# First layer's first norm: sums of squares and Newton steps moved from VectorE to GpSimd, and its statistics put ahead of the modulation blocks

## The chip, the core and the metric

The kernel runs on one core of one Trainium2 chip. The metric is the device time of one execution in microseconds. Of the kernel before there are three timed runs and one execution under the profiler. Engines are named as in the profile: PE (TensorE), DVE (VectorE), ACT (ScalarE), POOL (GpSimd), SP (SyncE, which only issues transfers here).

## The reference

One inference step of a two-layer diffusion trunk for 128 context tokens and 512 latent tokens (the kernel holds them as 640 columns), model width 1024. Cut to what the change touches:

```python
def _rms(x):
    xf = x.astype(F32)
    return xf * lax.rsqrt(jnp.mean(xf * xf, axis=-1, keepdims=True) + EPS)

def modulate(x, shift, scale):
    return (_rms(x) * (1.0 + scale.astype(F32)) + shift.astype(F32)).astype(x.dtype)

def modulation(cond, w_mod, b_mod):
    m = jax.nn.silu(cond) @ w_mod + b_mod
    m = m.reshape(m.shape[0], 1, N_MOD, D_MODEL)
    return tuple(m[:, :, i] for i in range(N_MOD))
```

Each layer computes the modulation (six vectors of 1024: shift, scale and gate for two sub-layers). Then it takes the modulated norm of the tokens and one input projection of it (`w_in`), whose columns go to three mixers side by side: a two-directional state-space scan, a latent attention and a gated MLP. An output projection and a gated residual follow, and then a second modulated norm and a gated convolutional feed-forward network (width 2816) with its residual.

## The kernel before

The residual stream `xT` lies in SBUF with the model dimension on the partitions: eight blocks (`KT`) of 128 rows by 640 token columns. Matmuls are made as three products of high and low halves (`mm3`, L146 to L148); the normed input is therefore two tiles, `hh` and `hl`.

**The modulation.** `mod_blocks` (L237 to L275) multiplies SiLU(cond), `sT`, with `w_mod`. For layer 0 it makes five blocks of 512 outputs here, each from four loads of 512 KB into tiles `raw` (L263, eight buffers in this stage), four products a load (L266). After a block, ACT copies its PSUM (`modev`, L272, one buffer); PE transposes it (`modt`, L152), DVE reduces it (`modred`, L245) and adds the bias (`mod`, L250, and L252 for the scales). The function is a generator: each `next` gives one of these twenty loads with its products.

**The norm.** `norm_stats` (L326) squares the eight blocks of `xT` on ACT (the first into `nacc`, L333, the others into `nsq`, L336, two buffers), adds seven times on DVE (L337), sums over the partitions with products against ones (`nst`, L346), makes `nv` on DVE (L349) and calls `rsqrt`: a first guess from the bits (`rs_y`, L104) and three Newton steps on DVE (L109, L111, L112: nine instructions). `bcast` then spreads the result as a diagonal (`dg`, DVE, L373) and products with ones (`nbc`, PE, L376). `norm_apply` goes through the eight blocks: `nt` (DVE, L358), `hh` (ACT, L362), `hl` (DVE, L363). The tokens are normed in two halves, columns 0 to 320 in `begin_layer` (L1676), 320 to 640 at the head of `mixers` (L847), whose `rest` makes the second half's broadcast and apply. `begin_layer` has, for layer 0,

```python
            for _ in range(8):
                next(modulate)
            r = self.norm_stats(N, 0, 320)
            for _ in range(2):
                next(modulate, None)
```

**What comes behind.** The input projection's part that gives tokens by rows is `wtok` (L905 to L907: wth·hh, wtl·hh, wth·hl), the part that gives columns is `win` (L146 to L148). Beside it the tables of the state-space scan are built: rotations `Tr` (POOL, complex products at L91 to L96, in chains, stored by a DMA `Td`, L673), products `G` (L91 to L96) and `Q` (L612 to L616) on DVE and POOL, and from `Q` the `tap` products on PE (L637 to L640), which ACT and DVE turn into `we` (L642, L643) and store. POOL's first rotation chain stands behind a memset of `uT` (L875). The scan's first instruction on DVE is `m` (L749).

**What sets the order.** The program is written in one stream; a scheduler puts each engine's instructions in an order of its own, by a simulated timeline, and that order is what the engine runs, one behind the other. So a small edit can move instructions far from it. Semaphores make an instruction wait for its inputs and for its buffers.

Of the kernel before, what the change touches and what calls it, by code (L numbers as in the profile page):

```python
# [14 lines left out]
OP = mybir.AluOpType  # L15
# [8 lines left out]
NT = 642  # L24
# [14 lines left out]
def spans(lo, hi):  # L39
    out = []  # L40
    if lo < 512:
        out.append((lo, min(hi, 512), 0))
    if hi > CX:
        out.append((max(lo, CX), hi, 1))
    return out


class Trunk:
# [263 lines left out]
                (nc.scalar if g else nc.sync).dma_start(out=dst[:, c], in_=o[:, c])  # L312


    def norm(self, pool, l, which, lo, hi, hh, hl):

        r = self.norm_stats(pool, lo, hi)

        def rest():
            pb = self.pz("nbc")  # L320
            self.bcast(pool, *r, pb)
            self.norm_apply(pool, l, which, lo, hi, hh, hl, pb)

        return rest

    def norm_stats(self, pool, lo, hi):  # L326

        nc = self.nc
        n = hi - lo
        acc = pool.tile([128, 322], F32, name=self.uid("nacc"), tag="nacc", bufs=2)  # L330
        for k in range(KT):
            if k == 0:
                nc.scalar.activation(acc[:, :n], self.xT[:, k, lo:hi], AF.Square)  # L333
            else:
                sq = pool.tile([128, 322], F32, name=self.uid("nsq"), tag="nsq", bufs=2)
                nc.scalar.activation(sq[:, :n], self.xT[:, k, lo:hi], AF.Square)  # L336
                nc.vector.tensor_tensor(acc[:, :n], acc[:, :n], sq[:, :n], op=OP.add)  # L337
        blocks = []
        for a, b, _ in spans(lo, hi):
            blocks += list(range(a, b - 127, 128))  # L340
            if (b - a) % 128:
                blocks.append(b - 128)
        nb = len(blocks)
        ps = self.pz("nst")
        for i, b in enumerate(blocks):
            nc.tensor.matmul(ps[:, i:i + 1], acc[:, b - lo:b - lo + 128], self.ones[:, 0:1],  # L346
                             start=True, stop=True)
        v = self.smt([128, nb], f"nv{nb}")
        nc.vector.tensor_scalar(v, ps[:, :nb], 1.0 / D, EPS, op0=OP.mult, op1=OP.add)  # L349
        return self.rsqrt(v, nb), [b - lo for b in blocks]  # L350

    def norm_apply(self, pool, l, which, lo, hi, hh, hl, pb):
        nc = self.nc
# [484 lines left out]
    def mixers(self, l, M, n1, N, hh, hl, fill):  # L838

        nc, V, A, I, tc = self.nc, self.nc.vector, self.nc.scalar, self.I, self.tc  # L840
# [3 lines left out]
        def mt(s, sh, dt=F32):  # L844
            return M.tile(list(sh), dt, name=self.uid(s), tag=s, bufs=1)

        rest = self.norm(N, l, 0, 320, NT, hh, hl)  # L847
        yc = mt("yc", [128, 5, 256])
        yA = mt("yA", [128, 2, NT])
        ssc = mt("ssc", [128, 5])  # L850
# [96 lines left out]
        v = win.tile([128, 5, 256], F32, name=self.uid("v"), tag="v")  # L947
        sq = win.tile([128, 256], F32, name=self.uid("vsq"), tag="vsq")
# [88 lines left out]
        for kt in range(6):  # L1037
            c = kt * 128 if kt < 5 else 128 + CX
            ps = self.pb("kv")
            for nb in range(2):  # L1040
                po = ps[:, nb]
                n = slice(nb * 512, (nb + 1) * 512)
# [12 lines left out]
        for tt in (4, 0, 1, 2, 3):  # L1055
            cs = slice(TOK[tt], TOK[tt] + 128)
            ps = self.pb("q")
            for nb in range(2):
                po = ps[:, nb, :384]
                n = slice(nb * 384, (nb + 1) * 384)  # L1060
# [25 lines left out]
        N = n2.enter_context(tc.tile_pool(name=f"n2{l}", bufs=1, side=sb))  # L1086
        fh, fl = self.norm_out(FH)
        self.project_b(l, vt, yh, yl, lambda: self.norm(N, l, 3, 0, 322, fh, fl)())
        rest = self.norm(N, l, 3, 322, NT, fh, fl)
# [585 lines left out]
    def begin_layer(self, l, modulate=None):  # L1675

        tc = self.tc
        self.sides = ("left", "right") if l == 0 else ("right", "left")
        es, n1 = ExitStack(), ExitStack()
        M = es.enter_context(tc.tile_pool(name=f"mix{l}", bufs=1, side=self.sides[0]))  # L1680
        hh, hl = self.norm_out(M)
        N = n1.enter_context(tc.tile_pool(name=f"n1{l}", bufs=1, side=self.sides[0]))
        if modulate:
            for _ in range(8):
                next(modulate)
            r = self.norm_stats(N, 0, 320)
            for _ in range(2):
                next(modulate, None)
            pb = self.pb("nbc")[:, 0]
            self.bcast(N, *r, pb)  # L1690
            for _ in modulate:
                pass
            self.norm_apply(N, l, 0, 0, 320, hh, hl, pb)
        else:
            self.norm(N, l, 0, 0, 320, hh, hl)()
        return es, n1, M, N, hh, hl
# [66 lines left out]
```

## Time and profile before

| | |
|---|---|
| Timed runs (3) | median 1823.65 us, 1820.12 to 1824.7 us |
| The profiled execution: its own time | 1824.9 us |
| Its span | 1823.1 us |
| PE busy | 1692.0 us (93%) |
| DVE busy | 1153.1 us (63%) |
| ACT busy | 680.8 us (37%) |
| POOL busy | 325.0 us (18%) |
| Mean granted TensorE clock | 0.949 of full speed |

The span is that of the trace, from the first instruction to the last; the execution's own time is 1.8 us longer, for what lies around it. It is 1.25 us above the median of the three runs. Busy shares are means over the whole span: in most of it (the feed-forward networks) PE has nine tenths and more; the change lies in the first 160 us, where the shares are others.

### The profile page before, as it was taken

Reading aid. Unit: us, or ns where it says so; the run is one execution under the profiler, and the core shown is the slowest. Engines: PE = TensorE matmul, PEld = TensorE weight load, DVE = VectorE, ACT = ScalarE, POOL = GpSimd, SP = SyncE. Lnnn points to the kernel's source line nnn. Section 1 sums busy time; section 2 is a strip of 40 time slices with the busy share of each in tenths; the row PEclk is TensorE's granted clock in tenths of the full one; section 3 lists DMA queues with packets and bytes.
Section 4 is the critical chain, followed back from the end, with each engine's and each line's share of the span. In section 5 each row is a group of like instructions: output and inputs, shape, how many; then the busy total and the mean of one; then the engine's idle time right before and its main releaser. Section 6 shows DMA issues by size and latency. Waiting matters only on the chain.

```text
span 1823.1 us, 28986 instructions
## 1 busy us (share of the span) xinstructions
PE 1692.0 (93%) x11248; PEld 1510.0 (83%) x11248; DVE 1153.1 (63%) x2377; ACT 680.8 (37%) x1210; POOL 325.0 (18%) x792
## 2 busy tenths in 40 slices
PE   5877889999999999999999878999989999999998
PEld 3767755469889999999999876455989999999998
DVE  6895875667674546456566568565786464555564
ACT  4343454433442424224244346343344132332241
POOL 2896300000186060540000130000000000000000
PEclk7888889899999999999999888989999999999999
DMA  9274453301443523223122543540223131321221
GB/s 283 85 186 119 132 164 123 114 13 58 129 146 116 162 56 117 72 85 110 37 88 67 161 109 105 169 132 1 70 70 93 36 104 47 93 90 39 82 82 58
DMA packets 217577, 182.48 MB, mean 100 GB/s; under 512 B 33438, under 2 KB 202204, under 8 KB 217440
## 3 DMA queue, kind: packets, MB, share of 16 engines
q1 hardware_dynamic: 194736, 154.33, 28.3%
q0 software_dynamic: 8272, 23.87, 4.5%
q10 hardware_dynamic: 14432, 2.44, 0.7%
q8 instruction: 89, 1.46, 0.3%
q14 instruction: 48, 0.39, 0.1%
HBM read 161.94 MB, written 18.64 MB: 99 GB/s over the span
## 4 chain that ended last, share of the span: by engine, by line
PE 74%; DVE 10%; DMA 7%; ACT 4%; issue 2%; POOL 2%; ACTq 0%; SPq 0%; DVEq 0%; POOLq 0%
PE up L146 11%; PE up L148 11%; PE up L147 10%; PE dn L146 5%; PE dn L148 5%; PE dn L147 5%; PE o L1294 3%; PE mod L266 2%; DMA raw<-w_mod 2%; PE wo L146 2%; PE wo L148 2%; PE wo L147 2%; DMA raw<-ffn_w_up 1%; PE s L1274 1%; DMA raw<-w_in 1%
## 5 line engine op out<-in xcount | busy, mean ns | idle before, releaser
L146 PE MATMUL up<-hh,whi 128*128 128x322 f32 x1408 | 435.1, 314 | 10.0 <-ACT hh L362 4.0
L148 PE MATMUL up<-hh,wlo 128*128 128x322 f32 x1408 | 438.1, 312 | 1.8 <-DVE wlo L123 1.5
L147 PE MATMUL up<-hl,whi 128*128 128x322 f32 x1408 | 436.9, 311 | 0.0
L146 PEld LDWEIGHTS up<-hh,whi 128*128 128x128 f32 x1408 | 264.9, 189 | 16.2 <-ACT whi L122 6.4
L148 PEld LDWEIGHTS up<-hh,wlo 128*128 128x128 f32 x1408 | 266.3, 189 | 4.0 <-DVE wlo L123 3.4
L147 PEld LDWEIGHTS up<-hl,whi 128*128 128x128 f32 x1408 | 267.2, 190 | 0.6 <-issue 0.4
L123 DVE TENSOR_TENSOR wlo<-raw,whi 128x1024 fp32r<-128x1024 f32 (+1 forms) x116 | 145.7, 1257 | 140.5 <-ACT whi L122 138.8
L148 PE MATMUL dn<-gh,dl 128*128 128x322 f32 (+1 forms) x704 | 217.9, 311 | 0.5 <-DVE dl L123 0.5
L147 PE MATMUL dn<-glo,dh 128*128 128x322 f32 (+1 forms) x704 | 218.0, 311 | 0.0
L146 PE MATMUL dn<-gh,dh 128*128 128x322 f32 (+1 forms) x704 | 209.9, 312 | 2.3 <-DVE cv L1548 1.8
L1508 DVE SCALAR_TENSOR_TENSOR xT<-dn,mod,xT 128x320 f32<-128x320 f32 (+2 forms) x288 | 112.1, 435 | 127.7 <-PE dn L148 127.6
L122 ACT CAST whi<-raw 128x1024 fp32r<-128x1024 f32 (+1 forms) x116 | 120.6, 1041 | 155.8 <-PE up L147 57.0
L1539 ACT ACTIVATE cv<-up,prm,cw 128x321 f32<-128x321 f32 x88 | 54.2, 620 | 246.7 <-PE up L148 244.4
L148 PEld LDWEIGHTS dn<-gh,dl 128*128 128x128 f32 x704 | 133.3, 189 | 0.7 <-DVE dl L123 0.7
L146 PEld LDWEIGHTS dn<-gh,dh 128*128 128x128 f32 x704 | 131.2, 190 | 2.8 <-issue 2.0
L147 PEld LDWEIGHTS dn<-glo,dh 128*128 128x128 f32 x704 | 133.0, 189 | 0.0
L1540 DVE SCALAR_TENSOR_TENSOR cv<-up,cw,cv 128x320 f32<-128x320 f32 x88 | 48.3, 549 | 63.8 <-ACT cv L1539 62.4
L266 PE MATMUL mod<-raw,sT 128*32 128x256 f32 x768 | 64.5, 432 | 23.4 <-DMA raw<-w_mod 21.4
L123 DVE TENSOR_TENSOR dl<-raw,dh 128x1024 fp32r<-128x1024 f32 x44 | 53.9, 1225 | 45.2 <-ACT dh L122 44.9
L122 ACT CAST dh<-raw 128x1024 fp32r<-128x1024 f32 x44 | 46.1, 1048 | 58.1 <-DMA raw<-ffn_w_down 50.0
L1257 DVE TENSOR_REDUCE nml<-mx 128x1 f32<-128x640 f32 x64 | 51.0, 820 | 23.9 <-PE mx L1255 23.6
L266 PEld LDWEIGHTS mod<-raw,sT 128*32 128x32 f32 x768 | 19.9, 115 | 53.0 <-DMA raw<-w_mod 25.5
(479 smaller groups left out, 3445.4 us busy)
## 6 DMA issues: line engine op xcount, KB each, us to landing
raw<-w_mod SPq DMA_DIRECT2D x96, 512.0 KB, 4.6
raw<-ffn_w_up SPq DMA_DIRECT2D x88, 512.0 KB, 4.0
raw<-ffn_w_down SPq DMA_DIRECT2D x44, 512.0 KB, 3.5
raw<-w_in SPq DMA_DIRECT2D x10, 512.0 KB, 6.5
we<-WEd POOLq DMA_DIRECT2D x8, 512.0 KB, 4.4
qt<-Qd POOLq DMA_DIRECT2D x8, 512.0 KB, 5.1
raw<-w_out SPq DMA_DIRECT2D x16, 256.0 KB, 5.3
raw<-w_out SPq DMA_DIRECT2D x8, 512.0 KB, 3.4
```

What stands on the lines that cost most here:

```text
L122: self.nc.scalar.copy(hi, raw)
L123: self.nc.vector.tensor_tensor(lo, raw, hi.bitcast(F32), op=OP.subtract)
L146: mm(ps, wh, xh, start=start, stop=False)
L147: mm(ps, wh, xl, start=False, stop=False)
L148: mm(ps, wl, xh, start=False, stop=stop)
L266: nc.tensor.matmul(ps[j * 32:j * 32 + 32, c0:c0 + 256], self.sT[:, k0 + j, :], rv[:, j, :], start=k0 == 0, stop=k0 == 4)
L1257: V.tensor_reduce(nm[:, tt:tt + 1], pb[:, :, :320], axis=AX.XY, op=OP.max, negate=True)
L1274: mm(ps, kh[i][:, kc_], qh[i], start=True, stop=False)
L1294: mm(pb[i * 64:(i + 1) * 64, 0], Vt[:, kt, 2 * p + i], Ps[i][kt], start=kt == 0, stop=kt == 4)
L1508: self.nc.vector.scalar_tensor_tensor(self.xT[:, m, a:b], po[:, a - lo:b - lo], self.modcol(l, gi, m, c), self.xT[:, m, a:b], op0=OP.mult, ...
L1539: A.activation(z[:, 0:321], po[:, 0:321], AF.Identity, bias=b, scale=c1)
L1540: V.scalar_tensor_tensor(z[:, 1:321], po[:, 0:320], c0, z[:, 1:321], op0=OP.mult, op1=OP.add)
```

## The change

`norm_stats` and `norm` take an engine `E`. With GpSimd, the seven additions and the Newton steps run there. `rsqrt` had a branch for GpSimd already, which has twelve instructions in place of nine (L109, L114, L115, L116, three times) and tile names with a `p` at the end (`rs_t3p`, `rs_y3p`); the first guess `rs_y03p` stays on DVE. Both halves of layer 0's first norm use it. In `begin_layer` the statistics are written ahead of all modulation loads, and ten loads stand between them and the broadcast. The other norms keep DVE. All sizes and formulas stay.

```diff
-    def norm(self, pool, l, which, lo, hi, hh, hl):
-
-        r = self.norm_stats(pool, lo, hi)
+    def norm(self, pool, l, which, lo, hi, hh, hl, E=None):
+
+        r = self.norm_stats(pool, lo, hi, E)
...
-    def norm_stats(self, pool, lo, hi):
+    def norm_stats(self, pool, lo, hi, E=None):

         nc = self.nc
+        E = E or nc.vector
...
-                nc.vector.tensor_tensor(acc[:, :n], acc[:, :n], sq[:, :n], op=OP.add)
+                E.tensor_tensor(acc[:, :n], acc[:, :n], sq[:, :n], op=OP.add)
...
-        return self.rsqrt(v, nb), [b - lo for b in blocks]
+        return self.rsqrt(v, nb, E), [b - lo for b in blocks]
...
-        rest = self.norm(N, l, 0, 320, NT, hh, hl)
+        rest = self.norm(N, l, 0, 320, NT, hh, hl, nc.gpsimd if l == 0 else None)
...
         if modulate:
-            for _ in range(8):
-                next(modulate)
-            r = self.norm_stats(N, 0, 320)
-            for _ in range(2):
+            r = self.norm_stats(N, 0, 320, self.nc.gpsimd)
+            for _ in range(10):
                 next(modulate, None)
```

The scheduler's orders around it. In the order's rows a name ends in its buffer's number, an operation is `output<-inputs`, and `x4` means four in a row. Lines of the changed kernel lie one higher than those of the kernel before from L329 on.

**Place 1, PE, from its first products with the modulation's weights.** Before:

```order
L266 MATMUL mod_452<-raw_474,sT 32x256 x4
L346 MATMUL nst_511<-ones,nacc_488 128x1 x3
L266 MATMUL mod_452<-raw_480,sT 32x256 x4
L266 MATMUL mod_530<-raw_531,sT 32x256 x4
L152 MATMUL modt_537<-ident,modev_486 128x128 x4
```

```order
L376 MATMUL nbc_551<-dg_552,ones 128x128 x3
L266 MATMUL mod_571<-raw_593,sT 32x256 x4
L266 MATMUL mod_571<-raw_599,sT 32x256 x4
L152 MATMUL modt_607<-ident,modev_605 128x128 x4
L346 MATMUL nst_679<-ones,nacc_656 128x1 x3
L905 MATMUL wtok_875<-wth_853,hh_418 128x288
```

Now:

```order
L152 MATMUL pa_325<-ident,rows_49_329 128x66
L347 MATMUL nst_448<-ones,nacc_425 128x1 x3
L266 MATMUL mod_470<-raw_471,sT 32x256 x4
L266 MATMUL mod_470<-raw_477,sT 32x256 x4
```

```order
L152 MATMUL modt_581<-ident,modev_572 128x128 x4
L906 MATMUL wtok_881<-wth_859,hh_418 128x288
L907 MATMUL wtok_881<-wtl_860,hh_418 128x288
...
L266 MATMUL mod_574<-raw_590,sT 32x256 x4
L908 MATMUL wtok_881<-wth_859,hl_419 128x288
...
L266 MATMUL mod_574<-raw_602,sT 32x256 x4
```

The first half's `nst` stood behind seven loads' products and stands now ahead of all twenty. The broadcast stood behind 18 loads' products and stands behind 11 now, followed by two more; 22 `wtok` products stand among the last three loads, where before all `wtok` products came behind the last load. On ACT, the third to seventh square of the first half (`nsq_433` to `nsq_445`) now stand behind four small loads `dcol` (L632); before, six of the seven stood ahead of those, and the seventh between them.

**Place 2, POOL and DVE, at the second half's Newton steps and broadcast.** POOL before (its first Newton row comes far behind these):

```order
L875 MEMSET uT_708 128x16
L573 MEMSET bs_1028 128x16
L625 MEMSET dcol_1086 128x1
L661 MEMSET Tr_1116 128x4
```

POOL now; between the rows that are shown lies the first rotation chain:

```order
L876 MEMSET uT_714 128x16
...
L91 TENSOR_TENSOR Tr_1122<-Tr_1122,rho 128x4
L93 TENSOR_TENSOR Tr_1122<-Tr_1122,rho 128x4
...
L109 TENSOR_TENSOR rs_t3p_690<-rs_y03p_688 128x3
...
L95 TENSOR_TENSOR G_1040<-G_1040,tm_186_1020 128x256
L96 TENSOR_TENSOR G_1040<-G_1040,tm_187_1021 128x256
L674 DMA Td_287<-Tr_1122 128x328
L674 DMA Td_288<-Tr_1122 128x328
L116 TENSOR_TENSOR rs_y3p_691<-rs_t3p_690,rs_y3p_691 128x3
```

DVE now, at the second half's broadcast:

```order
L364 SCALAR_TENSOR_TENSOR hl_419<-nt_646,mod_91,hh_418 128x320
L374 TENSOR_TENSOR dg_734<-ident,rs_y3p_691 128x384
L359 SCALAR_TENSOR_TENSOR nt_739<-xT,mod_91,nbc_733 128x192
L359 SCALAR_TENSOR_TENSOR nt_743<-xT,mod_91,nbc_733 128x128
L613 TENSOR_TENSOR tm_251_1636<-pw,CT_1633 128x288
```

The second half's twelve Newton instructions stand spread through POOL's first rotation chain, and the last of them behind the chain's two stores. DVE's `dg` needs that last one, and all that DVE does later stands behind `dg`. Ahead of the `uT` memset POOL now has 14 additions and the first half's twelve Newton instructions.

**Place 3, PE, at the last taps of the tables.** Before, they stood among the `win` products (19 products, 8 rows of taps, 26 products, 16 rows of taps):

```order
L640 MATMUL tap_1088<-Q_192_1049,bs_1028 32x112
L146 MATMUL win_2424<-hh_418,whi_2419 128x320
...
L148 MATMUL win_2511<-hh_418,wlo_2507 128x320
L637 MATMUL tap_1954<-Q_299_1941,bs_1894 32x112
```

Now:

```order
L638 MATMUL tap_1960<-Q_299_1947,bs_1900 32x112
...
L641 MATMUL tap_1094<-Q_192_1055,bs_1034 32x112
L1118 MATMUL gm_1587<-v_1420,wsT_1565 128x320
L1118 MATMUL gm_1592<-v_1420,wsT_1565 128x320
L146 MATMUL win_2430<-hh_418,whi_2425 128x320
```

All taps of layer 0 now stand ahead of the first `win` product of 320 columns.

## Rows read from the trace of the kernel before

**Rows 1.** The chain of work that ended last: shares of the span by engine.

```profile
PE 74%; DVE 10%; DMA 7%; ACT 4%; issue 2%; POOL 2%; ACTq 0%; SPq 0%; DVEq 0%; POOLq 0%
```

**Rows 2.** Windows: length, busy PE, PEld, DVE, ACT, POOL, PEclk, DMA, GB/s.

```profile
25.00:50.00 25.00, 17.33 (x130) 6.30 (x130) 23.64 (x110) 7.60 (x15) 0.00 (x0) 0.62 1.09 349
75.00:100.00 25.00, 21.77 (x147) 18.71 (x147) 23.77 (x72) 10.70 (x34) 21.86 (x73) 0.93 0.29 86
125.00:150.00 25.00, 19.22 (x153) 18.08 (x154) 17.28 (x36) 8.85 (x23) 21.30 (x49) 0.86 0.58 149
```

**Rows 3.** DVE's groups by line and shape, 15 to 70 us: busy, mean ns.

```profile
L337 DVE TENSOR_TENSOR nacc<-nacc,nsq 128x322 f32<-128x322 f32 x7 | 3.4, 487 | 0.2 <-ACT nsq L336 0.2
L337 DVE TENSOR_TENSOR nacc<-nacc,nsq 128x320 f32<-128x320 f32 x7 | 3.4, 483 | 1.2 <-ACT nsq L336 1.1
L109 DVE TENSOR_TENSOR rs_t<-rs_y 128x3 f32<-128x3 f32 x6 | 1.2, 208 | 0.0
```

**Rows 4.** Timeline, first norm and modulation: start, length, instruction, [idle before <-releaser].

```profile
25.19 1.08 PE L266 MATMUL mod<-raw,sT 128*32 128x256 f32 x8 [5.22 <-DMA raw<-w_mod]
29.30 1.02 ACTq L631 DMA_DIRECT2D dcol<-ssm_d  x2
30.36 0.83 ACT L336 ACTIVATE nsq<-xT 128x322 f32<-128x322 f32 x2 [0.66 <-DVE nacc L337]
36.67 1.44 PE L346 MATMUL nst<-ones,nacc 128*128 128x1 f32 x6 [0.45 <-DVE modred L245]
50.38 1.06 PE L376 MATMUL nbc<-dg,ones 128*128 128x128 f32 x6 [1.85 <-DVE dg L373]
51.36 1.94 PE L266 MATMUL mod<-raw,sT 128*32 128x256 f32 x16
57.01 0.44 PE L905 MATMUL wtok<-wth,hh 128*128 128x288 f32 x1
57.25 0.44 PE L906 MATMUL wtok<-wtl,hh 128*128 128x288 f32 x1
```

**Rows 5.** Timeline of POOL, first rotation chain and products G.

```profile
53.39 0.12 POOL L875 MEMSET uT<- 128x16 f32 x1 [2.05 <-PE mod L266]
53.70 1.41 POOL L91 TENSOR_TENSOR Tr<-Tr,rho 128x4 f32<-128x4 f32 x1
55.52 0.20 POOL L92 TENSOR_TENSOR tr<-Tr,rho 128x4 f32<-128x4 f32 x1
66.23 0.65 POOL L91 TENSOR_TENSOR G<-pw,bb 128x256 f32<-128x256 f32 x1
73.60 0.85 POOL L96 TENSOR_TENSOR G<-G,tm 128x256 f32<-128x256 f32 x1
124.71 0.95 POOL L96 TENSOR_TENSOR G<-G,tm 128x256 f32<-128x256 f32 x1
```

**Rows 6.** Timeline of POOL, the same Newton steps in another norm.

```profile
178.56 0.32 POOL L115 TENSOR_SCALAR rs_t5p<-rs_t5p 128x5 f32<-128x5 f32 x1
178.96 0.25 POOL L116 TENSOR_TENSOR rs_y5p<-rs_t5p,rs_y05p 128x5 f32<-128x5 f32 x1
```

**Rows 7.** Timeline of DVE, the second half's broadcast and apply.

```profile
64.74 0.66 DVE L373 TENSOR_TENSOR dg<-ident,rs_y 128x384 f32<-128x384 f32 x1
68.73 0.67 DVE L358 SCALAR_TENSOR_TENSOR nt<-xT,mod,nbc 128x192 f32<-128x192 f32 x2 [2.72 <-PE nbc L376]
72.13 2.47 DVE L363 SCALAR_TENSOR_TENSOR hl<-nt,mod,hh 128x192 fp32r<-128x192 f32 x2 [2.73 <-ACT hh L362]
```

**Rows 8.** Timeline, the last taps on PE and what DVE makes of them.

```profile
138.12 0.58 PE L637 MATMUL tap<-Q,bs 128*32 128x112 f32 x2 [5.78 <-POOL Q L616]
145.68 0.24 DVE L643 SCALAR_TENSOR_TENSOR we<-id,dcol,we 128x16 f32<-128x16 f32 x1 [5.22 <-ACT we L642]
153.11 0.23 DVE L643 SCALAR_TENSOR_TENSOR we<-id,dcol,we 128x16 f32<-128x16 f32 x1 [5.20 <-ACT we L642]
157.25 0.83 DVE L749 TENSOR_TENSOR m<-E,T 128x656 f32<-128x656 f32 x1
```

## The prediction

> **What bounds the kernel now.** I read the chain of waits first, then windows of 25 us over the stretch that the change touches, then the timelines of its engines. PE has 74% of the chain [rows 1], but that is the mean of the span. At 25 to 50 us another picture stands [rows 2]: PE is busy 17.33 of 25 us at a granted clock of 0.62, between the two levels 1.2 and 2.4 GHz; DVE is busy 23.64; the transfers run at 349 GB/s. Here loads of `w_mod` and DVE set the pace. From 75 to 100 us DVE (23.77) and POOL (21.86) are both nearly full, and at 125 to 150 us POOL still has 21.30 while DVE has fallen to 17.28. Those two build the tables of the scan, and PE waits for them: a tap waits 5.78 us for POOL's Q [rows 8]. So up to the scan's first instruction at 157.25 us [rows 8] the end is set by two queues, DVE's and POOL's, and what is put late on either shows in the time unless a later wait gives way. Behind the scan come the feed-forward networks, where PE is full and nothing can be made up.
>
> **DVE gets lighter.** Its fourteen additions take 483 to 487 ns each, 6.8 us together, and eighteen Newton instructions at some 208 ns add 3.7 [rows 3]; these durations overlap a little, so the queue gains perhaps 7.5 us. All of that lies before 66 us. It shortens the end only if what DVE does next is there earlier, and the next points say that it is not.
>
> **PE starts later.** The first product of the modulation runs at 25.19 us [rows 4], as its load lands. Now the first half's `nst` stands ahead of it, and that needs seven additions on POOL, whose third to seventh square stand behind four `dcol` loads on ACT. Before, the last two of these were issued from 29.30 for 1.02 us, to 30.32 [rows 4]; a `dcol` waits there for other transfers, not for anything that the change removes. One square is 0.83 / 2, some 0.45 us [rows 4]. The additions on POOL have no row; the nearest are additions and products of 256 columns, 0.65 us, 0.85 and, with DVE busy beside them, 0.95 [rows 5]. By 320/256 that is 0.81 to 1.19 us. I take 0.85, since the first few of them have little beside them, and keep both ends: five additions are 4.05 to 5.95, taken 4.3. Since `nsq` has two buffers, the squares cannot run ahead. 30.3 + 0.45 + 4.3 = 35.1, then `nst`, 1.44 [rows 4]: the first modulation product at 36.5, 11.3 late. PE had idled for loads before, 7.7 of the 25 us [rows 2], and by 36.5 the eight buffers are full; that recovers part. The work that PE did from 25.19 to 53.30 (the end of the last modulation products, 51.36 + 1.94) is 17.33 - 1.44 for `nst`, + 1.06 + 1.94 [rows 2, 4] = 18.9 us. To that come the 22 `wtok` products that stand among the last loads now, at 57.25 - 57.01 = 0.24 each [rows 4], 5.3. The last modulation product thus ends at T0 = 36.5 + 18.9 + 5.3 = 60.7, where it was 53.3: 7.4 late. Bounds: 55, if loads and clock run as well as they can (twelve loads of 512 KB behind the first eight are 18 us at 349 GB/s, from 37.5), and 64, if PE stays at its lower clock throughout or `wtok` waits for `hl`.
>
> **The second half's norm.** POOL's `uT` memset waits for that last product (53.39 before) and its chain with the G products ends at 73.60 + 0.85 = 74.45 [rows 5], 21.1 us later. Now twelve Newton instructions stand in this chain; on POOL one takes 0.25 us, or 0.40 from start to start [rows 6], 0.20 for the chain's own small ones [rows 5]: 2.4 to 4.8, I take 2.6, for most stand between others of the same length. The first operation of the chain took 1.41 and not 0.20 us [rows 5]; that start was paid earlier now, with the first addition: -1.2. So the chain and the last Newton step end at 60.7 + 21.1 + 2.6 - 1.2 = 83.2. On POOL that is 8.7 late for all its later work. On DVE `dg` comes then; it ran at 64.74 [rows 7]. With 0.66 for `dg`, 1.06 for `nbc` [rows 4], 0.67 for two `nt` and 0.5 for `hh`, the first `hl` of the second half is at 86.1; before, 72.13 [rows 7]. DVE's queue behind it is 14.0 late: the 7.5 us won are spent as a wait.
>
> **What gives way.** Before, DVE waited 5.22 and 5.20 us at two `we` [rows 8], because their taps stood among `win` products on PE; those taps stand ahead of all of them now, so these waits can close. If one does, DVE's 14.0 becomes 8.8; POOL's 8.7 stays, since its own idle is small. Both queues then arrive 8.7 late at the scan. The sum: 1824.9 + 8.7 = 1833.6 for the profiled execution, which lies 1.25 above the median; so **1832.4 us**. A measurement of this kernel tells about 0.3% (5.5 us) from no change.
>
> The unknown ends around it: T0 from 55 to 64 is -5.7 to +3.3, the Newton steps -0.2 to +2.2, and 0 or both waits closed instead of one is +5 or, as far as POOL lets it, nothing. That case has 0.38 with 1829 to 1840.
>
> **Rivals.**
>
> 1. *No change: all of it is absorbed* (0.25). For it: DVE has 7.7 and POOL 3.7 us idle from 125 to 150 us [rows 2], the two `we` waits are 10.4, and PE's tap wait of 5.78 [rows 8] is a wait for the same queues. If T0 comes at 57 and POOL's rows, which stretched from 0.65 to 0.95 with DVE beside them [rows 5], run faster while DVE waits, POOL is 3 late and DVE 9 - 10.4, and the time is 1824.9 - 1.25 + 0 to 3, about 1825. Against it: DVE and POOL are full from 75 to 100 us, so nothing is taken back there.
>
> 2. *Faster: the taps' new place decides* (0.15). Both `we` waits close, 10.4 us off DVE, and the second norm is no more than some 5 late, since T0 is at 55 and POOL's chain loses its stretch. Then the scan comes 10.4 - 5 = 5.4 earlier and the time is 1818.2. It decides this way if the second `dg` runs before 72 us or so and POOL's last Q is not later than before. Against it: T0 at 55 with 21 us of POOL behind it puts `dg` at 77; it needs the chain to shrink by 5.
>
> 3. *POOL's last table comes later still* (0.12). POOL's last Q stands behind more of its fourth rotation chain than before; PE waited for POOL at the taps already [rows 8], and now all `win` products queue behind that. Some 6.5 us more of chain on top of 8.7: about 1839.
>
> 4. *DVE and POOL shut each other out* (0.10). In the rows an operation on one engine is only stretched by the other: POOL's G products took 0.65 to 0.95 [rows 5], and no DVE row stood still for a whole POOL instruction. The Trainium skill ("SBUF — State Buffer", section "SBUF: two separate sides") says otherwise: the port pair that the two share is locked for a whole instruction, and the loser, such as a DVE operation with two SBUF inputs against a POOL operation that reads SBUF, blocks fully. As a mechanism of this kernel: if each of the fourteen additions of 0.85 us held up DVE's queue for its length, DVE would lose 12 us where it gained 7.5, the first half's `dg` would come some 3 us later than PE is ready for it, and `wtok` and the last loads with it. T0 would be 63.7 and the time 1835.4. DVE is busy 23.64 of 25 us there [rows 2], so nothing would hide it; for it speaks also that the stretch exists at all.
>
> **How the numbers follow.** The forecast, 3 and 4 are slower, 0.60 together; no change has 0.25, faster 0.15. The likeliest value is 1832.4. The range reaches down to rival 2 with a little beside it, 1817, and up over rival 3, 1841; it leaves out T0 late with rival 3 at once, and a larger gain than 7 us, for which I see no row.
>
> **What would show it.** Right: PE's first `mod` near 36 us and not 25; the `uT` memset on POOL near 60; second `dg` on DVE near 83 with a long wait for POOL's last L116; the two waits before `we` smaller; the scan's first `m` near 166. DVE's busy time from 25 to 50 us falls, and it buys nothing. Wrong: a first `mod` before 32 us (then the squares did not wait for `dcol`, or the additions are cheaper); a T0 below 56; a second `dg` before 75; or an `m` at 157 or earlier although `dg` is late, which would mean that the tables' end was set by something that I have not seen, a transfer for instance.

## The result and the profile after

The changed kernel takes 1846.45 us (median of four runs, 1841.82 to 1850.85) against 1821.88 for the kernel before beside it: a ratio of 1.0136, 95% interval 1.0112 to 1.0160, so 20 to 29 us slower. The forecast had the sign and the chain of steps up to 84 us, and a third of the size: 8.7 us, 1832.4, with 1841 as the upper end. The profiled execution took 1848.79 us (span 1847.0).

The same windows as [rows 2], of the kernel after:

```profile
25.00:50.00 25.00, 9.78 (x98) 5.08 (x98) 24.97 (x83) 8.30 (x17) 18.21 (x24) 0.62 0.86 272
75.00:100.00 25.00, 13.66 (x71) 10.85 (x70) 14.68 (x40) 6.99 (x20) 23.12 (x71) 0.86 0.15 49
125.00:150.00 25.00, 15.05 (x117) 13.45 (x117) 20.37 (x32) 8.68 (x26) 24.49 (x48) 0.86 0.85 220
```

From 25 to 50 us PE does 9.78 us of work in place of 17.33, and DVE is no emptier for what it lost, but fuller: 24.97. From 75 to 100 us DVE, full before, falls to 14.68; it waits for POOL. From 125 to 150 us POOL has no gap left, while PE and its 19.22 have become 15.05.

The steps on their engines, from the timelines of the kernel after (start, length, instruction, [idle before <-releaser]); they answer to [rows 4, 5, 7]:

```profile
37.42 1.44 PE L347 MATMUL nst<-ones,nacc 128*128 128x1 f32 x6 [18.19 <-POOL nacc L338]
38.79 4.49 PE L266 MATMUL mod<-raw,sT 128*32 128x256 f32 x40
63.11 0.13 POOL L876 MEMSET uT<- 128x16 f32 x1 [12.26 <-PE mod L266]
83.33 0.56 DVE L374 TENSOR_TENSOR dg<-ident,rs_y3p 128x384 f32<-128x384 f32 x1 [13.80 <-POOL rs_y3p L116]
```

PE's first `mod` stood at 25.19 and was forecast at 36.5; it is at 38.79. `uT` went from 53.39 to 63.11 (forecast 60.7), the second `dg` from 64.74 to 83.33 (forecast 83.2), with the wait of 13.80 us for POOL in front of it. Up to here the forecast holds to 2.5 us. That `dg` comes on the number itself is luck: `uT` is 2.4 us late, and from `uT` to `dg` it takes 20.2 us in place of the 22.5 forecast. Now the last tables, which answer to [rows 8], first on POOL:

```profile
116.14 1.15 POOL L674 DMA_DIRECT2D Td<-Tr  x2 [0.30 <-POOL Tr L96]
123.36 0.10 POOL L662 MEMSET Tr<- 128x4 f32 x1 [6.08 <-DMA Td<-Tr]
156.72 2.05 POOL L617 TENSOR_TENSOR Q<-tm,tm 64x288 f32<-64x288 f32 x2
```

POOL stood still for 6.08 us until the stores `Td` of its third chain had ended, before it could begin the fourth. In the kernel before it made Q products in that time; now all of the last Q products stand behind the fourth chain's start. POOL's last Q ends at 158.8, before at 139.1. DVE's last Q ends at 159.1, before at 146.9, and by the profile it is for one of DVE's that PE's late taps wait (first the row of the kernel before, then two of the kernel after):

```profile
145.95 0.94 DVE L616 TENSOR_TENSOR Q<-tm,tm 64x288 f32<-64x288 f32 x2
...
157.66 1.43 DVE L617 TENSOR_TENSOR Q<-tm,tm 64x288 f32<-64x288 f32 x2
158.25 0.55 PE L638 MATMUL tap<-Q,bs 128*32 128x112 f32 x2 [3.82 <-DVE Q L617]
```

So both engines' last tables come at about the same time. Then DVE, from the last two `we` to the scan, with some rows between:

```profile
163.06 0.23 DVE L644 SCALAR_TENSOR_TENSOR we<-id,dcol,we 128x16 f32<-128x16 f32 x1 [3.21 <-ACT we L643]
165.17 0.23 DVE L644 SCALAR_TENSOR_TENSOR we<-id,dcol,we 128x16 f32<-128x16 f32 x1 [1.87 <-ACT we L643]
...
173.32 0.36 DVE L1136 TENSOR_TENSOR krg<-kra,k_normr 128x192 f32<-128x192 f32 x1 [2.74 <-ACT vsq L1126]
...
174.61 0.55 DVE L990 SCALAR_TENSOR_TENSOR ckl<-win,prm,ckh 128x320 fp32r<-128x320 f32 x1
...
175.87 0.55 DVE L984 SCALAR_TENSOR_TENSOR cql<-win,prm,cqh 128x320 fp32r<-128x320 f32 x1
176.34 0.83 DVE L750 TENSOR_TENSOR m<-E,T 128x656 f32<-128x656 f32 x1
```

The two waits before `we` did shrink, from 10.4 us to 5.1, so that the last `we` is only 12.1 us late. But `m`, which followed 4.1 us behind it before, follows 11.2 us behind now: DVE's order has put operations of the attention (`krg`, `ckl`, `cql`) ahead of it. Of the 7.0 us that this adds, 2.7 are the wait of `krg` for ACT's `vsq`, 3.0 are the operations from `krg` to `cql`, and the rest lies ahead of `krg`. The `win` products, which PE used to make between the taps, now come behind them (PE's timeline, the same stretch); DVE shows no wait for them ahead of `ckl` or `cql`:

```profile
164.67 1.34 PE L1118 MATMUL gm<-v,wsT 128*128 128x320 f32 x4
165.61 0.55 PE L146 MATMUL win<-hh,whi 128*128 128x320 f32 x1
...
174.68 0.31 PE L146 MATMUL win<-hh,whi 128*128 128x320 f32 x1
```

So `m` is 19.1 us late, PE's first product `o` of the attention 19.3 (308.8 for 289.5), and the last `o` of layer 1 23.4 (1289.0 for 1265.6). A single execution tells such steps only to some 5 us: e16 and e18 below are one kernel, and in their profiled executions `m` is at 152.3 and 156.3, the first `o` at 283.0 and 286.2, and from the first `o` to the last 971.0 and 976.2 us pass.

### The profile page after: what moved, and what is told of

It is laid out like the page before. It is cut to its first block, busy times and chain, and to the rows that moved or that the text cites. A ratio compares the mean times of both kernels' runs of the same rounds, so it can differ in the third digit from the quotient of the medians.

```text
span 1847.0 us, 28995 instructions
## 1 busy us (share of the span) xinstructions
PE 1686.8 (91%) x11248; PEld 1505.5 (82%) x11248; DVE 1155.1 (63%) x2345; ACT 681.2 (37%) x1210; POOL 341.6 (18%) x830
## 5 line engine op out<-in xcount | busy, mean ns | idle before, releaser
L123 DVE TENSOR_TENSOR wlo<-raw,whi 128x1024 fp32r<-128x1024 f32 (+1 forms) x116 | 147.7, 1274 | 149.2 <-ACT whi L122 148.2
L146 PE MATMUL wo<-yh,whi 128*128 128x322 f32 (+1 forms) x192 | 60.3, 321 | 2.2 <-ACT yh L122 1.8
```

Source lines behind the costliest of these rows:

```text
L123: self.nc.vector.tensor_tensor(lo, raw, hi.bitcast(F32), op=OP.subtract)
L146: mm(ps, wh, xh, start=start, stop=False)
```

## The experiments

Four theories. **A**: the second half's Newton steps, spread in POOL's chain, make DVE wait and hold up the tables. **B**: PE's late start costs. **C**: DVE and POOL hinder each other. **D**, formed behind the first four runs: the scheduler's new order of everything else costs, whatever was moved.

This table gathers all runs: the time of two instructions in the profiled execution (the scan's first `m` on DVE and the attention's first `o` on PE), and the timed medians. A run's ratio is to the kernel before, run on the same chip beside it.

| run | first m | first o | median us | ratio, 95% interval |
|---|---|---|---|---|
| before | 157.3 | 289.5 | 1818.84 to 1823.81 | |
| the change | 176.3 | 308.8 | 1846.45 | 1.0112 to 1.0160 |
| e1 place alone | 163.1 | 306.3 | 1833.63 | 1.0046 to 1.0096 |
| e2 second half on DVE | 156.2 | 308.7 | 1835.43 | 1.0054 to 1.0109 |
| e3 additions alone | 163.2 | 312.0 | 1851.35 | 1.0129 to 1.0211 |
| e4 second half alone | 171.3 | 307.0 | 1843.17 | 1.0093 to 1.0163 |
| e5 moved work, old order | 174.9 | 305.4 | 1836.37 | 1.0071 to 1.0136 |
| e6 old work, new order | 172.1 | 308.1 | 1840.08 | 1.0094 to 1.0144 |
| e7 Newton steps ahead of chain | 180.0 | 313.7 | 1850.64 | 1.0155 to 1.0204 |
| e8 neutral shuffle | 149.2 | 299.6 | 1839.18 | 1.0089 to 1.0146 |
| e9 new front, old rest | 175.8 | 309.5 | 1841.48 | 1.0073 to 1.0167 |
| e10 shuffled front, old rest | 157.7 | 292.0 | 1817.23 | 0.9944 to 1.0003 |
| e11 old front, new rest | 165.9 | 300.4 | 1834.07 | 1.0058 to 1.0109 |
| e12 first half, old rest | 157.3 | 291.3 | 1818.37 | 0.9963 to 1.0016 |
| e13 as e9, fourth chain behind | 171.0 | 305.3 | 1834.89 | 1.0053 to 1.0122 |
| e14 second half, old rest | 168.7 | 300.3 | 1829.77 | 1.0043 to 1.0090 |
| e15 place, old rest | 157.5 | 287.5 | 1821.06 | 0.9983 to 1.0038 |
| e16 shuffled front to the scan | 152.3 | 283.0 | 1816.25 | 0.9961 to 1.0018 |
| e17 new front to the second we | 171.7 | 302.4 | 1829.44 | 1.0028 to 1.0060 |
| e18 (e16 again) | 156.3 | 286.2 | 1816.99 | 0.9957 to 0.9993 |

### Parts of the change, each with the order that the scheduler finds for it (e1 to e4)

e1 keeps only the new place; both halves are on DVE:

```diff
-            r = self.norm_stats(N, 0, 320, self.nc.gpsimd)
+            r = self.norm_stats(N, 0, 320)
...
-        rest = self.norm(N, l, 0, 320, NT, hh, hl, nc.gpsimd if l == 0 else None)
+        rest = self.norm(N, l, 0, 320, NT, hh, hl)
```

> Undoes the engine change in both halves: additions and Newton steps on DVE again, the statistics still written ahead of the modulation loads. Theory A (the time is lost through the second half's Newton steps, which stand in POOL's first rotation chain, so that DVE's second dg and POOL's tables come late): dg before 70 us, the scan's first m within 5 us of 157, time within 5 us of the kernel before. Theory B (it is lost through PE's late start, because nst stands ahead of the modulation products and waits for the additions): nst is first on PE here too, first mod near 32 us, and the time is 6 to 10 us above the kernel before.

e2 takes only the second half back to DVE (the last two lines of that edit):

> The changed kernel, but with the second half's norm on DVE. PE's late start stays: first mod near 38 us, uT memset near 62. Theory A: no wait of DVE for POOL's last Newton step, second dg at 73 to 76 us, most of the 24 us gone, time 0 to 9 us above the kernel before. Theory B: the late start is what costs, time 15 to 25 us above the kernel before.

e3 leaves the additions on POOL and the Newton steps on DVE (`self.rsqrt(v, nb)` in place of `self.rsqrt(v, nb, E)`):

> The changed kernel, but with the Newton steps of both halves on DVE; the fourteen additions stay on POOL. First mod near 38 us again, uT memset near 62, and each addition still 1.4 us beside DVE's two-input operations. Theory A: as in the run before, 0 to 9 us above the kernel before. Theory B, and a theory C by which the shared port makes the additions cost DVE what it loses: 15 to 25 us above.

e4 has the old place, the first half on DVE, the second on POOL (`self.norm_stats(N, 0, 320)` behind eight blocks):

> The kernel before, with the second half's norm alone on POOL; the first half and its place as before. PE starts as early as before, first mod near 25 us. Theory A: second dg behind POOL's rotation chain at 77 to 80 us, the fourth rotation chain ahead of POOL's Q products, scan's first m 10 to 16 us late, time 10 to 18 us above the kernel before. Theory B: within 4 us of the kernel before.

None comes near the kernel before, and the parts do not add up: 13, 15, 31 and 23 us by the ratios, 24.6 for the whole. e1's 9.8 us are what theory B had said. But in e2, where PE's first `mod` stands as late as 39.6, the tables are not late at all: `m` is at 156.2, and yet `o` is 19.2 us late. What is lost there, is lost behind the tables, where the edit does nothing. That made theory D.

### Work and order apart (e5, e6, e7, e8)

To hold the order fixed, e5 and e6 trace a second kernel first, take each engine's instructions in the order that the scheduler gave that one, and tie those of their own in this order by dependencies without semaphores:

```diff
+            for p, q in zip(row, row[1:]):
+                tc.add_manual_dep(q, p.name, no, reason="order")
```

e5 has the change's work on POOL in the order of the kernel before:

> The 14 additions and 24 Newton steps are on POOL as in the change, but every other instruction of every engine stands in the order of the kernel before (PE begins with the mod matmuls, POOL runs its fourth rotation chain behind the first Q products); POOL's moved instructions stand where the change has them, ahead of the chain and between its steps. Theory D (what costs is the new order of all that stands behind the norm): first mod at 25, second dg at 75 to 78, POOL's last Q at 143 to 147, and 1826 to 1832 us. Theory A (the second half's norm inside POOL's chain costs by itself): what is lost at the second dg (some 11 us) stays lost, 1836 to 1846 us.

e6 has all of the norm on DVE in the order of the change:

> All additions and Newton steps are on DVE as before, but the matmuls, loads, table and scan instructions of every engine stand in the order that the changed kernel has. Theory D: second dg back at about 65, and still 1836 to 1843 us, most of the change's loss. Theories A and C (the work on POOL costs): POOL is freed of 38 instructions, its last Q comes at 140 to 145, and the time is 1828 to 1833 us.

e7 is the change with POOL's first chain held behind the second half's Newton steps:

```diff
-            self.ssm_rotations(0, ssm, nc.gpsimd, 4, ("hq", "ys"))
+            with tc.issue_after(newton2):
+                self.ssm_rotations(0, ssm, nc.gpsimd, 4, ("hq", "ys"))
```

> The changed kernel, with POOL's first rotation chain held in the order until the second half's last Newton step is issued; POOL's fourth chain falls back behind the first Q products. Theory A: second dg at 66 to 70 in place of 83, POOL's last Q at 146 to 150 in place of 159, and 1833 to 1840 us. Theory D: the loss behind the scan stays, 1841 to 1848 us.

e8 moves no work: the kernel before with one number changed in `begin_layer`:

```diff
-            for _ in range(8):
+            for _ in range(9):
...
-            for _ in range(2):
+            for _ in range(1):
```

> The kernel before with its norm statistics asked for behind 9 of the 10 modulation blocks in place of 8: same engines, same work, only the order that the scheduler then finds differs in some hundred places on POOL and DVE. Theory D: an order found anew costs by itself, 1829 to 1840 us. Theories A, B and C: nothing they speak of is changed, 1820 to 1827 us.

e6 loses as D said, though POOL has none of the norm. e8 is the clearest: nothing is moved, its tables are early (timeline of DVE), and it is 16 to 27 us slower:

```profile
142.20 0.26 DVE L643 SCALAR_TENSOR_TENSOR we<-id,dcol,we 128x16 f32<-128x16 f32 x1 [0.53 <-ACT we L642]
149.17 0.83 DVE L749 TENSOR_TENSOR m<-E,T 128x656 f32<-128x656 f32 x1
```

Its `m` is 8.1 us ahead of the kernel before and its `o` 10.1 behind. PE's waits between show where some of it goes: products `glu` wait 9.8 us for ACT, where the longest such wait in the kernel before is 0.22 us; beside these, `y` waits 8.0 us for loads of `tp` (1.4 before) and `kt` 5.0 for DVE (0.9 for ACT before). The two at `glu`:

```profile
236.96 2.51 PE L829 MATMUL glu<-gl,wg 128*128 128x320 f32 x4 [2.68 <-ACT gl L824]
246.55 6.34 PE L829 MATMUL glu<-gl,wg 128*128 128x320 f32 x12 [7.08 <-ACT gl L824]
```

e7 missed what I expected of its time under either theory. It brought the second `dg` from 83.3 to 71.1 and POOL's last Q from 158.8 to 145.7, as A wanted, and lost both again: in the order found for it, `m` stands behind even more of the attention, at 180.0. e5 went against my expectation for D: with every other instruction in the old order it lost 13 to 25 us. Its own timelines tell why. On POOL:

```profile
29.55 0.86 POOL L345 TENSOR_TENSOR nacc<-nacc,nsq 128x320 f32<-128x320 f32 x1 [7.25 <-ACT nsq L344]
...
108.45 0.54 POOL L705 DMA_DIRECT2D we<-WEd  x1 [9.30 <-DMA WEd<-we]
```

The second `dg` (86.5) holds up all of DVE behind it; among that is a `we` whose store POOL waits for, 9.30 us, before it may issue a load, and its third and fourth chains stand behind the load. DVE late makes POOL late. So work and order both cost, and theory A is a part of it.

### One order up to a point, another behind it (e9 to e18)

The next kernels take the order of one kernel up to a given instruction of DVE and that of another for the rest. A kernel is told by four values, here those of e9. In the first three stand the blocks ahead of the statistics and whether the first and the second half are on POOL; `CUT` names the fourth `we` addition. Only the norm's own additions and Newton steps are left to the scheduler; all else is tied.

```diff
+THIS, FRONT, REST = (0, True, True), (0, True, True), (8, False, False)
+CUT = ("DVE", ("id16",), 3)
...
+    rest = [k for k in old(REST)[1] if k not in set(front)]
```

e9, the change up to the fourth `we`, then the old order:

> The changed kernel, with every engine's instructions behind the layer's last table (the fourth we addition on DVE) put back into the order of the kernel before; up to there the order and the engines are those of the change. Theory D, first half (the new order behind the tables costs): last we at about 165 as in the change, first m at 167 to 171 in place of 176, attention's first o matmul at 300 to 304 in place of 309, and 1832 to 1838 us. If the tables' delay is the whole cause: first o still at 307 to 310 and 1843 to 1849 us.

e10, the same with e8's front (`THIS`, `FRONT` = (9, False, False)):

> The neutral shuffle again (all the norm's work on DVE, one modulation block more ahead of the statistics), with its own order up to the last we and the order of the kernel before behind it. Its tables came 11 us earlier than those of the kernel before (last we at 142 in place of 153) and its time was 1839. Theory D: what it lost, it lost behind the tables, so first m at 146 to 150, first o at 279 to 284, and 1812 to 1818 us, faster than the kernel before. If the scan and the attention wait for something else than the tables (loads of weights, the clock): first o stays at 288 to 291 and 1819 to 1825 us.

e11, the reverse (`THIS`, `FRONT` = (8, False, False), `REST` = (0, True, True)):

> The kernel before up to its last we addition, engines and order, and behind that the order of the changed kernel. Theory D: last we at 153 as before, first m at 160 to 165, first o at 296 to 303, and 1829 to 1836 us. If only the delay of the tables costs: 1820 to 1826 us.

e12, half the change (`THIS`, `FRONT` = (8, True, False)):

> Half of the change at the old place: the first half's additions and Newton steps on POOL, asked for behind 8 modulation blocks, the second half on DVE; its own order up to the last we, the order of the kernel before behind it. The first dg comes at 50 to 52 and the second at 63 to 67 as before, POOL's rotations start at 55 to 60. If work on POOL costs only where DVE waits for its last step (theory A): last we at 150 to 157 and 1818 to 1827 us. If POOL's delay itself costs (its rotations start later by up to 7 us): last we at 157 to 162 and 1827 to 1833 us.

e11 has no work moved and its tables in time, and pays 11 to 20 us for the order behind. DVE's timeline shows the same rows ahead of `m` as in the change, 10.2 us from the first `gt` behind the last `we` to `m`, where the change has 10.8:

```profile
153.10 2.65 DVE L653 SCALAR_TENSOR_TENSOR we<-id,dcol,we 128x16 f32<-128x16 f32 x1 [5.04 <-ACT we L652]
...
163.03 0.36 DVE L1145 TENSOR_TENSOR krg<-kra,k_normr 128x192 f32<-128x192 f32 x1 [2.73 <-ACT vsq L1135]
...
165.42 0.55 DVE L993 SCALAR_TENSOR_TENSOR cql<-win,prm,cqh 128x320 fp32r<-128x320 f32 x1
165.88 0.83 DVE L759 TENSOR_TENSOR m<-E,T 128x656 f32<-128x656 f32 x1
```

Yet PE has its 45 `win` products here at their old place, between the taps:

```profile
140.25 0.64 PE L152 MATMUL win<-hh,whi 128*128 128x320 f32 x1
...
149.73 0.38 PE L647 MATMUL tap<-Q,bs 128*32 128x112 f32 x2
```

So it is DVE's order, and not the new place of those products, that puts `m` so far behind the last `we`.

e10 gets back all that e8 had lost, 1839 to 1817, by the rest's order alone. Its rows missed what I expected, though, `m` at 157.7 for 146 to 150 and `o` at 292.0 for 279 to 284: `m` waited 8.9 us for POOL's copy to `E`. But e9 stays at 13 to 30 us with `m` at 175.8, so my expectation of 167 to 171 failed, for two reasons. The last `we` is 11.5 us late, which no order behind it can mend; and where two orders are joined, a wait arises that neither had (the seam). In e9, e13 and e14 it is this one, on DVE just ahead of `m` (here of e9):

```profile
174.20 0.49 DVE L1130 TENSOR_TENSOR gt<-gm,gvb 128x320 f32<-128x320 f32 x1 [7.01 <-PE gm L1127]
```

PE's `gm` products stand there behind `win` products. So the times of these three are upper ends of what their fronts cost. e12, with a seam of 3.9 us, says that the first half's work on POOL is free. Its additions and DVE's operations hinder each other there as in the change (an addition takes 1.39 us in the median, for 0.86), so theory C costs nothing that can be measured in the first half.

Open was then which part of the front made it 18 us late. e13 is e9 with POOL's fourth chain taken out of the front's order, so that it stands behind the last Q:

```diff
+    front = [k for k in front if not (k[0].endswith("Pool") and f"({tr}_" in text[k])]
```

> As e9 (the change's engines and order up to the last we, the order of the kernel before behind it), but POOL's fourth rotation chain stands behind the last Q products instead of among them. If that place is what makes POOL's last table later than the change's work explains: POOL's last Q from 153.0 to 143 to 147, first m from 175.8 to 166 to 170, first o from 309.5 to 299 to 304, and 1829 to 1836 us, near the sum of the prediction. If the late second dg on DVE decides all the same: m at 173 to 176 and 1838 to 1844 us.

e14, the second half alone (`THIS`, `FRONT` = (8, False, True)):

> The other half of the change at the old place: the second half's additions and Newton steps on POOL, the first half's on DVE; its own order up to the last we, the order of the kernel before behind it. Theory A (DVE waits for POOL's last Newton step and what stands behind it comes late): second dg at 75 to 79, last we at 158 to 164, first m at 166 to 172, 1832 to 1839 us, against 1818 for the first half alone. If e4's loss lay in its order behind the tables: 1820 to 1827 us.

e15, the place alone (`THIS`, `FRONT` = (0, False, False)):

> The new place alone: the statistics asked for ahead of the modulation blocks, all on DVE; its own order up to the last we, the order of the kernel before behind it. PE's first mod at 32. If PE's late start is covered and e1's loss (1833.6) lay behind the tables: last we at 148 to 154, first m at 155 to 159, 1818 to 1826 us. If the late start costs (theory B): first m at 161 to 165 as in e1 and 1828 to 1834 us.

e16, e10 with the cut at the scan's second `m`:

> As e10, but the shuffled order is kept up to the scan's first two products m instead of the last we; in e10 the first m waited 8.9 us for POOL's copy to E, which the old order has behind other loads. If the tables set the end: first m at 147 to 151, first o at 281 to 286 and 1807 to 1814 us, faster than the kernel before. If something else holds the attention: first o at 288 to 292 and 1815 to 1822 us.

With the rest held in the old order the parts come apart. The place alone, with PE's first `mod` at 30.8 in place of 25.2: nothing to be measured, and theory B falls. (Its last `we` is 5.5 us early, which a seam takes back: `m` waits 8.6 us for POOL's copy to `E`. Its start is 5.6 us late and the change's 13.6, but e2's was 14.4 late, and its tables were in time.) The first half: nothing. The second half: 8 to 16 us, less than I expected, the seam's 7.0 among them as far as they last to the end. Its Newton steps look to be what does it: where they are on DVE and the additions on POOL (e3) the second `dg` is at 71.6, in the change at 83.3. In e14 DVE's row has the cause, theory A:

```profile
75.86 0.56 DVE L384 TENSOR_TENSOR dg<-ident,rs_y3p 128x384 f32<-128x384 f32 x1 [11.58 <-POOL rs_y3p L123]
```

In e13 POOL's last Q ends at 147.5, 8.4 late, and the last `we` comes 6.6 late, as DVE's timeline of e13 has it:

```profile
159.72 0.23 DVE L654 SCALAR_TENSOR_TENSOR we<-id,dcol,we 128x16 f32<-128x16 f32 x1 [2.32 <-ACT we L653]
...
170.97 0.83 DVE L760 TENSOR_TENSOR m<-E,T 128x656 f32<-128x656 f32 x1
```

e9, with the same seam, has 154.9, 164.6 and 175.8: the fourth chain's place is worth 7.4 us at the last Q and 4.8 at `m`. The 4.8 are little more than what the two executions of one kernel differ by at `m` (4.0), and the times of e9 and e13 are not clear of each other. Of the 13.7 us that `m` still comes late, 6.6 stand at the last `we`; the rest is the seam, which exists because the `win` products no longer stand between the taps. e17 therefore puts the cut at the second `we`, ahead of the last taps (`CUT = ("DVE", ("id16",), 1)`, the fourth chain out of the front as in e13), and e18 is e16 in more executions:

> All of the change's work on POOL and its early place, with the change's order only up to the second of the layer's four we additions; from there the order of the kernel before, so that PE has its 45 win products between the last taps again and POOL its fourth chain behind the first Q products. This is the case that the prediction's sum describes: nothing behind the late second norm in another order. If the rest of the loss came by the order: second dg at 82 to 83 as in the change, POOL's last Q at 145 to 148, first m at 164 to 168, first o at 296 to 301, and 1826 to 1832 us. If the moved work itself costs more than the 8.7 us of the sum: first m at 170 or later and 1834 to 1842 us.

> The kernel of e16 once more, in more rounds, since its interval (0.9961 to 1.0018) could not tell 7 us from nothing. If its first o at 283 (289.5 before) is kept to the end: a ratio of 0.994 to 0.998. If later stages give it back: 0.998 to 1.001.

e17 is all of the change's work at its early place, and 5 to 11 us slower, where the change has 20 to 29. So, by the times, the order from the second `we` on, with the fourth chain's place, is the larger part of the loss. (Its profiled execution, at 1844.1, is the longest of its eight, the others took 1825.9 to 1830.8, so its rows are to be read with care.) That its time is near the 8.7 us of the sum is luck, for the rows do not follow the sum: POOL's last Q, which begins at 150.9, `m` and `o` miss what I expected of them (`m` is where the other reading put it), and on DVE's timeline of e17 stands:

```profile
160.06 0.23 DVE L654 SCALAR_TENSOR_TENSOR we<-id,dcol,we 128x16 f32<-128x16 f32 x1 [5.80 <-ACT we L653]
167.58 0.24 DVE L654 SCALAR_TENSOR_TENSOR we<-id,dcol,we 128x16 f32<-128x16 f32 x1 [5.28 <-ACT we L653]
171.68 0.83 DVE L760 TENSOR_TENSOR m<-E,T 128x656 f32<-128x656 f32 x1
```

Both waits stay at their old 5 us, so that DVE's 14 us arrive whole at `m` (+14.4) and `o` is 12.9 late. By these rows the order from there on is worth 4.7 us at `m` and 6.4 at the first `o`; the rest of the some 17 us between e17 and the change lies behind the first `o` or in the difference of single executions, and which stays open. It stays open, too, why the median keeps only 5 to 11 us where this execution is 12.9 late at the first `o` and 16.6 at the last.

e18 settles the other question. With all work on DVE, the last `we` 4 to 8 us earlier by the shuffled front, and the old order from the scan on, the kernel takes 1816.99 us against 1820.75, a ratio of 0.9957 to 0.9993: 1 to 8 us faster than the kernel before. The first `o` was 3.3 to 6.5 us earlier in the two executions.

## Why the prediction was wrong in size

**Right.** DVE's relief buys nothing; PE starts some 11 us late (13.6) and ends its modulation late; the second half's Newton steps in POOL's chain set `dg` at 83; DVE loses all it had won as one wait. The sign follows from these. The place (e15) and the first half (e12) cost nothing that can be measured, the whole 5 to 11 us (e17), the second half alone 8 to 16 with a seam (e14): so it is the second half that costs, as the argument had it.

**The first step that failed: "On POOL that is 8.7 late for all its later work".** I carried the lateness through POOL's old order, though the order had changed. POOL's time from `uT` to the end of its last Q went from 85.7 us to 95.7. Grouped from its timeline by the steps from start to start, 24 more instructions of the fourth chain, which now stand ahead of the last Q, take 7.7 us; the waits grow by 4.8, the 6.08 above the largest; the Newton steps take 2.2 (forecast 2.6); and the first three chains take 5.0 less (forecast 1.2 less). All else makes 0.3. With 9.7 at `uT` that makes 19.7 us, not 8.7. Rival 3 named this mechanism with its place, and priced it at 6.5 us; beside the forecast it is 11 at the last Q, of which 7.4 went with the fourth chain's place (e13 against e9). Its chance of 0.12 was too low: that the fourth chain stood ahead of the Q products was to be read in the order, and that a chain waits for the stores of the one before it stood in the old trace, with 0.31 and 0.92 us at its second and third.

**The second: "Both queues then arrive 8.7 late at the scan".** The waits ahead of the two `we` closed by half, as I took it. But the sum ends at the last `we`, 12.1 us late, and takes the way from there to `m` as unchanged. DVE's new order put `krg`, `ckl` and `cql` ahead of `m`, and DVE lost 7.0 us there, more than the 5.3 that the waits had given. e11 shows the same rows with the `win` products still between the taps, so the taps' new place is not the cause.

**What was not in the sum at all** is the order behind the last table. "Behind the scan come the feed-forward networks, where PE is full and nothing can be made up" is no reason that nothing is lost: e8 loses 16 to 27 us and e11 11 to 20 with their tables in time. Shown is the whole: from the second `we` on, the change's order, with its place for the fourth chain, costs what lies between e17 (5 to 11 us) and the change (20 to 29). How much of it each of the three places has in the change's time is not: e9 and e13 hold a seam, and a delay of the tables covers some of the order behind it.

**Rival 4** came true in kind, in the window where it could; the last part has its rows. It added to the first steps, not a time of its own: five additions took 7.6 us and not 4.3, and PE's first `mod` and `uT` came 2.3 and 2.4 us behind the forecast. What it costs later, where both engines build the tables, no run separates. I had written that no DVE row stood still for a whole POOL instruction in the old trace. That was a misreading: there a small product of DVE takes 0.77 us in place of 0.18 as POOL begins its Q products,

```profile
119.36 0.18 DVE L94 TENSOR_TENSOR tm<-B,sf 128x32 f32<-128x32 f32 x1
119.40 1.68 POOL L616 TENSOR_TENSOR Q<-tm,tm 64x288 f32<-64x288 f32 x2
119.48 0.77 DVE L95 TENSOR_TENSOR bb<-bb,tm 128x32 f32<-128x32 f32 x1
```

and the 1.41 us of the first chain's first operation, which I took for a start that is paid once, lie beside products of DVE that run without a gap from 53.53 to 54.97. I had also expected that DVE's busy time from 25 to 50 us falls; it rose to 24.97, as the blocked time counts as busy.

**Rivals 1 and 2** needed the tables in time; `dg` at 83 excluded both.

## What to carry to other kernels

Where a scheduler sets the order, an edit has two effects, its work and the order that is found anew, and the second can be the larger: one number in a loop, with no work moved, cost 16 to 27 us here. So read the new order of every engine to the end of what waits, look for what now stands ahead of the instruction that the next stage waits for, and before judging an edit hold the order fixed and try it again. And moving work to an idle engine does not help where the busy engine's next instruction needs the result: the first half's norm was free on POOL, the second half's was not, since it stood in a chain that DVE then had to wait for, 11.6 to 14 us.

## What the runs showed of the hardware

DVE and POOL exclude each other for whole instructions. The timeline of the kernel after, where five of POOL's additions meet DVE:

```profile
29.76 7.61 POOL L338 TENSOR_TENSOR nacc<-nacc,nsq 128x320 f32<-128x320 f32 x5 [9.51 <-ACT nsq L337]
29.78 0.18 DVE L399 SCALAR_TENSOR_TENSOR eq<-eq,er 128x32 f32<-128x32 f32 x1
...
30.55 0.88 DVE L399 SCALAR_TENSOR_TENSOR eq<-eq,er 128x32 f32<-128x32 f32 x1
31.35 0.41 DVE L433 SCALAR_TENSOR_TENSOR ss<-ss,sz 128x256 f32<-128x256 f32 x1
31.69 0.41 DVE L437 SCALAR_TENSOR_TENSOR sc<-sc,sz 128x256 f32<-128x256 f32 x1
32.02 0.88 DVE L404 TENSOR_TENSOR eq<-eq,ep 128x32 f32<-128x32 f32 x1
32.82 0.41 DVE L433 SCALAR_TENSOR_TENSOR ss<-ss,sz 128x256 f32<-128x256 f32 x1
```

Where DVE stands idle beside it (e5, at 29.55) an addition takes 0.86 us, what I had taken. Against the full DVE these five take 7.61, 1.52 each. In the rows shown one small DVE operation in three takes 0.88 in place of 0.18, that is, stands still for most of one addition, and the two behind it run undisturbed at 0.41. From one such operation to the next it is 1.47 us, the 0.86 of an addition and 0.6 more, so it seems that the next addition waits meanwhile; its own start is not shown. The Trainium skill ("SBUF — State Buffer", section "SBUF: two separate sides") says of the port pair that the two engines share that it is an exclusive lock for a whole instruction, and names DVE operations with two SBUF inputs against a POOL operation that reads SBUF. The rows agree with it, and give the price in both directions: 0.70 us for the DVE operation, 0.66 for the mean of these five additions.
